# A hybrid RG-LRU and attention block: when the last two column tiles of x are read out, and where a weight's low part stands on VectorE

## The chip, the cores and the metric

The kernel runs on one core of a Trainium2 chip. The metric is the device time of one execution in microseconds (us). Engines are named as in the profile: PE is TensorE's matmuls and PEld its weight loads, DVE is VectorE, ACT is ScalarE, POOL is GpSimd, SP is SyncE, which here only issues DMAs. L503 is line 503 of the kernel.

## The reference, cut to what matters

One encoder layer over 512 positions of width 1024. The part around the change is the input projection, the four-tap depthwise convolution on its first 512 columns, and the two gates of the recurrence:

```python
h = rms_norm(x, attn_norm_g)
proj = h @ w_in
xr, gate, q, k, v = jnp.split(proj, [...], axis=-1)      # 512 columns each
y = b                                                     # centred depthwise convolution
for k in range(4):
    y = y + xp[:, k:k + S] * w[k]
# RG-LRU, forward and backward, each with its own gates; 8 blocks of 64 columns
r = sigmoid(einsum('bsnc,ncd->bsnd', xb, wa) + ba)
i = sigmoid(einsum('bsnc,ncd->bsnd', xb, wx) + bx)
a = exp(-8 * softplus(-lam) * r)
b_in = sqrt(1 - a * a) * (i * x)
# scan, gate with GeLU, dilated attention on q, k, v, two output projections,
# an MLP of width 4096 with squared ReLU, and a last RMSNorm
```

## The kernel before, in words

Every large matmul is made three times in a reduced-precision form of float32: each operand is split into a high part (`hi`) and a rest (`lo`), and `mm3` adds hi*hi, hi*lo and lo*hi (L333, L334, L335). Weights arrive by SP in chunks of 128x1024 (512 KB) into `wraw`, three buffers. `conv_hi(i)` makes chunk i's high part `whi`, on ACT (L277), or on DVE (L275) for chunks 7, 8 and 9. `conv_lo(i)` subtracts on DVE to make `wlo` (L285), which frees the `wraw` buffer, and asks SP for the next chunk (`emit_dma`, L241). Chunk 3 is the fourth column tile of x's weights, chunks 4 to 7 are V's, chunks 8 to 11 are the gate's.

Activations lie transposed: columns of the projection on the 128 partitions, the 512 positions along the free dimension. x's 512 columns are four tiles t = 0..3 (`pxr[t]`), each in a PSUM bank of its own. PSUM has eight banks; four are named `pj`, and `pxr[0..3]` take all four. The next users of these four are the four gate products `pg[0..3]` of a call of `lru_gates`, so a `pg` matmul has to wait until the `pxr` tile in its bank has been read out, and in the next call until ACT has read out the `pg` before it.

For each tile t the code has these steps:

- `conv_a(t)`: DVE reads `pxr[t]` out of PSUM and scales it into `xr` (L503), and ACT makes of it the convolution's first term `xc` (L505).
- `conv_b(t)`: three dependent DVE instructions add the other taps (L510, L511, L512), and SP copies the two halves of `xc` into each other's partitions (`xcs`, L522, two DMAs).
- `lru_gates(t)`: sixteen small matmuls (L531) from `xc` into four `pg` tiles, in the order 0, 2, 1, 3, and four sigmoids on ACT (L534) in the same order. The first sigmoid of the kernel has a load of ACT's function table ahead of it.

`xmm(ks)` issues the matmuls of x's fourth tile for the given parts k of the contraction. After them PE makes V in 32 steps n (three matmuls each; eight steps to a chunk, so step 8 is the first that uses chunk 5). `lru_gates(0..3)` stand behind steps 5, 8, 11 and 14; `conv_b(2)` behind step 2, `conv_b(3)` and `conv_lo(6)` behind step 6, `conv_hi(7)` and `conv_lo(7)` behind 7, `conv_hi(8)` and `conv_lo(8)` behind 12.

PE, ACT, DVE and POOL issue in the order in which the code is written. SP's order is laid out by the framework's planner. Each of them issues in order, so an instruction that waits holds up what stands behind it.

The lines that the change touches, as they are:

```python
xmm((0, 1))
rstd = row_tile(rcol, "et")
conv_a(0, pxr[0])
conv_a(1, pxr[1])
conv_hi(5)
cneg, chalf = next(spc)          # POOL: the last small constants
...                              # POOL: three DMA issues
xmm((2, 3, 4))
conv_b(0)
conv_lo(5)
conv_a(2, pxr[2])
xmm((5, 6))
conv_b(1)
conv_hi(6)
xmm((7,))
conv_a(3, pxr[3])
```

So DVE's order here is xr(0), xr(1), conv_b(0), wlo(5), xr(2), conv_b(1), xr(3), conv_b(2), conv_b(3), wlo(6), and ACT's is xc(0), xc(1), whi(5), xc(2), whi(6), xc(3), then the sigmoids.

Of the kernel before, what the change touches and what calls it, by code (L numbers as in the profile page):

```python
# [109 lines left out]
def hybrid_kernel(ctx: ExitStack, tc, xw, xn, w_in, w_v, w_out, w_up, w_dn, gates, vecs, rel, onehot, fg, out):  # L110
# [13 lines left out]
    def g_(name, dt=FT, shape=(P, S)):  # L124
        return work.tile(list(shape), dt, name=name, tag="g", bufs=NG)
# [4 lines left out]
    def ps_(name, tag):  # L130
        return psum.tile([P, S], FT, name=name, tag=tag, bufs={"pj": 4, "gs": 2, "et": 2}[tag])

    def f(t):
        return t.bitcast(FT)
# [5 lines left out]
    def vec(n, i):  # L140
        return vt[:, VEC[n] + i:VEC[n] + i + 1]
# [77 lines left out]
    def ublock(h, b, f):  # L219
        return w_up[h * HF + f + {"11": 0, "12": 1, "21": 2, "22": 3}[b]]  # L220
# [8 lines left out]
    def oblock(b, half=1):  # L229
        return w_out[int(half), int(b[1]) - 1, int(b[0]) - 1]  # L230

    def wblock(h, b, q):
        return w_dn[h, int(b[1]) - 1, (int(b[0]) - 1) * NQ + q]
# [3 lines left out]
    def emit_dma():  # L237
        if plain:
            i = plain.popleft()
            r = stream.tile([P, 1024], FT, name="wraw", tag="wraw", bufs=3)  # L240
            nc.sync.dma_start(r, source(chunks[i]))  # L241
            raws[i] = r
# [19 lines left out]
    def neg_next(i):  # L262
        conv_neg(i, stream.tile([P, 1024], FR, name="wlo", tag="wlo", bufs=4))

    def conv_hi(i):
        if i < len(chunks):
            i = swap.get(i, i)
            hi = stream.tile([P, 1024], FR, name="whi", tag="whi", bufs=4)
            if i + 1 == BY_DMA[2]:
                neg_next(i + 1)  # L270
            splits[i] = (hi,)
            if i in BY_DMA:
                splits[i] += (negs.pop(i),)
            if i in ON_DVE:
                nc.vector.tensor_copy(hi, raws[i])  # L275
            else:
                act(hi, raws[i], AF.Copy)  # L277

    def conv_lo(i):
        if i < len(chunks):  # L280
            i = swap.get(i, i)
            r = raws.pop(i)
            if i not in BY_DMA:
                lo = stream.tile([P, 1024], FR, name="wlo", tag="wlo", bufs=4)
                nc.vector.tensor_tensor(lo, r, f(splits[i][0]), op=OP.subtract)  # L285
                splits[i] += (lo,)
            c = chunks[i]
            if isinstance(c, tuple) and c[0] in ("o", "r"):
                if c[1][0] != "s":
                    emit_dma()  # L290
                elif c == ("r", "s2"):
                    nc.gpsimd.dma_start(r, oblock("21", 0), accum_op=OP.add)
                    raws[C_WO + RSEQ.index("s4")] = r
            elif isinstance(c, tuple) and len(c) == 4:
                h, kind, f0 = c[:3]
                if kind == "t1" and cq[h, f0, "t2"] not in raws:
                    nc.gpsimd.dma_start(r, ublock(h, "22", f0), accum_op=OP.add)
                    raws[cq[h, f0, "t2"]] = r
                elif kind == "22":
                    t = raws[cq[h, f0, "t3"]]  # L300
                    nc.vector.tensor_tensor(t, t, r, op=OP.add)
                elif kind in ("t2", "21"):
                    held[kind] = r
                    if len(held) == 2:
                        t = held.pop("t2")
                        nc.vector.tensor_tensor(t, t, held.pop("21"), op=OP.add)
                        raws[cq[h, f0, "t4"]] = t
                        emit_dma()
                if kind in ("11", "22"):
                    emit_dma()  # L310
            elif isinstance(c, tuple) and c[1][0] == "s":
                nxt = {"s1": ("s2", "22"), "s2": ("s4", "21")}.get(c[1])
                if nxt:
                    raws[cd_[c[0]] + {"s2": 2 * NQ + 2 * c[2], "s4": 6 * NQ + c[2]}[nxt[0]]] = r
                    if (c[0], c[1]) != (1, "s2"):
                        nc.gpsimd.dma_start(r, wblock(c[0], nxt[1], c[2]), accum_op=OP.add)
            else:
                emit_dma()
# [13 lines left out]
    def mm3(o, a, b, first, last, on=False):  # L332
        nc.tensor.matmul(o, lhsT=a[0], rhs=b[0], start=bool(first), stop=False, skip_group_check=on)  # L333
        nc.tensor.matmul(o, lhsT=a[0], rhs=b[1], start=False, stop=False, skip_group_check=on)  # L334
        nc.tensor.matmul(o, lhsT=a[1], rhs=b[0], start=False, stop=bool(last), skip_group_check=on)  # L335
# [66 lines left out]
    def hk(k):  # L402
        return (h_hi[:, k, :], h_lo[:, k, :])

    def wk(c, k):
        if c < 3:
            return tuple(t[:, c * P:(c + 1) * P] for t in w3[k])
        hi, lo = splits[c]
        return (hi[:, k * P:(k + 1) * P], lo[:, k * P:(k + 1) * P])
# [31 lines left out]
    pxr = {t: ps_("pxr", "pj") for t in range(3)}  # L441
# [59 lines left out]
    def conv_a(t, pp):  # L501
        xr = g_("xr")
        nc.vector.tensor_tensor(xr, pp, rstd, op=OP.mult)  # L503
        c = g_("xc")
        act(c, xr, AF.Identity, scale=vec("w2", t), bias=vec("cb", t))  # L505
        xrt[t], xc[t] = xr, c

    def conv_b(t):
        xr, c = xrt.pop(t), xc[t]
        stt(c[:, 2:], xr[:, :S - 2], vec("w0", t), c[:, 2:], op0=OP.mult, op1=OP.add)  # L510
        stt(c[:, 1:], xr[:, :S - 1], vec("w1", t), c[:, 1:], op0=OP.mult, op1=OP.add)  # L511
        stt(c[:, :S - 1], xr[:, 1:], vec("w3", t), c[:, :S - 1], op0=OP.mult, op1=OP.add)  # L512
        xcs[t] = swapped("xcs", c)
# [5 lines left out]
    def swapped(name, t):  # L519
        o = g_(name)  # L520
        for b in range(2):
            nc.sync.dma_start(o[halves[1 - b]], t[halves[b]])  # L522
        return o
# [134 lines left out]
    def xmm(ks):  # L658
        for k in ks:
            mm3(pxr[3], wk(3, k), hk(k), k == 0, k == KD - 1)  # L660
# [4 lines left out]
    rstd = row_tile(rcol, "et")  # L665
    conv_a(0, pxr[0])
    conv_a(1, pxr[1])
    conv_hi(5)
    cneg, chalf = next(spc)
    nc.gpsimd.dma_start(relt, rel)  # L670
# [1 line left out]
        nc.gpsimd.dma_start(oht[i], onehot[:, BCOL[i]])  # L672
    xmm((2, 3, 4))
    conv_b(0)
    conv_lo(5)
    conv_a(2, pxr[2])
    xmm((5, 6))
    conv_b(1)
    conv_hi(6)
    xmm((7,))  # L680
    conv_a(3, pxr[3])


    scans = deque()
# [1177 lines left out]
```

## Time and profile before

| what | value |
|---|---|
| median of 3 runs | 528.62 us (528.49 to 528.72) |
| profiled execution | 528.4 us, its span 526.6 us |
| granted TensorE clock, mean | 0.997 |
| busy: PE, PEld, DVE, ACT, POOL | 519.5, 446.8, 431.0, 361.1, 67.5 us |
| V's first step on PE | starts at 28.57 us of the span |
| the four groups of gate matmuls | start at 32.74, 37.11, 41.67 and 45.82 us |

The span is the time from the first instruction to the last; the 1.8 us around it are not in the trace. Matmuls overlap: a matmul row lasts some 0.39 us, but the next one starts 0.23 us later. Where PE is followed closely, the distance between starts counts and not the duration. DVE and ACT rows overlap a little in the same way, by up to 0.1 us.

### The profile page before, as it was taken

To read this page: it belongs to the slowest core of one execution; us is meant where nothing else is said; L and a number is where in the kernel's file an instruction comes from. 1 tells how busy PE (TensorE), PEld (TensorE's weight loads), DVE (VectorE), ACT (ScalarE), POOL (GpSimd) and SP (SyncE) were. 2 spreads that over 40 slices of the span, in tenths; PEclk is the share of its full clock that TensorE was granted. 3 is DMA by queue.
4 is the path that set the end of the run, shared out by engine and by line. 5 is a ranking of instruction groups with operands and counts; after the bars stand their busy time and mean duration, and the time that the engine had idled before them with its cause. 6 is when DMAs were issued, how large, how long until landed. Compare 5 with 4: busy or idle time off the path is not lost.

```text
span 526.6 us, 9183 instructions
## 1 busy us (share of the span) xinstructions
PE 519.5 (99%) x3495; PEld 446.8 (85%) x3495; DVE 431.0 (82%) x710; ACT 361.1 (69%) x570; POOL 67.5 (13%) x96
## 2 busy tenths in 40 slices
PE   9999999999999999999999999999999999999995
PEld 7866888787877888899999888888999999888884
DVE  5799589778789898898779987889756977987885
ACT  7577967777878958585577755566477677656654
POOL 1631000001002121001300132001101300213000
PEclk9999999999999999999999999999999999999998
DMA  8888155585478999948494999976978496899604
GB/s 308 285 210 221 41 158 160 172 153 180 91 241 178 315 223 256 356 153 200 118 225 137 241 265 273 281 300 160 288 232 201 115 228 202 219 276 250 149 1 159
DMA packets 35739, 108.29 MB, mean 206 GB/s; under 512 B 4109, under 2 KB 7082, under 8 KB 35696
## 3 DMA queue, kind: packets, MB, share of 16 engines
q1 hardware_dynamic: 26000, 74.67, 41.1%
q0 software_dynamic: 8784, 31.76, 32.5%
q10 hardware_dynamic: 912, 1.28, 1.3%
q8 instruction: 27, 0.44, 0.4%
q14 instruction: 16, 0.13, 0.1%
HBM read 98.24 MB, written 4.21 MB: 195 GB/s over the span
## 4 chain that ended last, share of the span: by engine, by line
PE 98%; DMA 1%; DVE 0%; ACT 0%; issue 0%; ACTq 0%
PE pu L335 10%; PE pu L334 10%; PE pu L333 10%; PE pd L334 10%; PE pd L333 10%; PE pd L335 10%; PE pqk L333 3%; PE pqk L335 3%; PE pqk L334 3%; PE pt L853 2%; PE pav L940 2%; PE pxr L446 2%; PE pv L333 2%; PE pg L531 2%; PE pn L799 1%; PE pv L335 1%
## 5 line engine op out<-in xcount | busy, mean ns | idle before, releaser
L285 DVE TENSOR_TENSOR wlo<-wraw,whi 128x1024 fp32r<-128x1024 f32 x72 | 87.8, 1220 | 24.7 <-ACT whi L277 24.5
L277 ACT ACTIVATE whi<-wraw 128x1024 fp32r<-128x1024 f32 x69 | 72.9, 1058 | 36.1 <-PE pd L335 21.6
L334 PE MATMUL pd<-wlo,ah 128*128 128x512 f32 (+1 forms) x195 | 75.2, 386 | 0.0
L333 PE MATMUL pd<-whi,ah 128*128 128x512 f32 (+1 forms) x195 | 75.2, 386 | 0.0
L335 PE MATMUL pd<-whi,al 128*128 128x512 f32 (+1 forms) x195 | 75.2, 386 | 0.0
L277 ACT ACTIVATE whi<-tw 128x1024 fp32r<-128x1024 f32 x40 | 42.3, 1059 | 37.7 <-DMA tw<-in_w_up_dram 10.7
L285 DVE TENSOR_TENSOR wlo<-tw,whi 128x1024 fp32r<-128x1024 f32 x40 | 48.9, 1222 | 18.6 <-ACT whi L277 18.6
L334 PE MATMUL pu<-hl,whi 128*128 128x256 f32 x224 | 63.4, 283 | 0.0
L335 PE MATMUL pu<-hh,wlo 128*128 128x256 f32 x224 | 63.4, 283 | 0.0
L333 PE MATMUL pu<-hh,whi 128*128 128x256 f32 x224 | 63.4, 283 | 0.0
L333 PE MATMUL pu<-h2h,whi 128*128 128x256 f32 (+1 forms) x200 | 60.1, 300 | 0.0
L335 PE MATMUL pu<-h2h,wlo 128*128 128x256 f32 (+1 forms) x200 | 60.0, 300 | 0.0
L334 PE MATMUL pu<-h2l,whi 128*128 128x256 f32 (+1 forms) x200 | 60.0, 300 | 0.0
L333 PEld LDWEIGHTS pu<-hh,whi 128*128 128x128 f32 x224 | 43.0, 192 | 0.0
L334 PEld LDWEIGHTS pu<-hl,whi 128*128 128x128 f32 x224 | 43.0, 192 | 0.0
L335 PEld LDWEIGHTS pu<-hh,wlo 128*128 128x128 f32 x224 | 43.0, 192 | 0.0
L333 PEld LDWEIGHTS pd<-whi,ah 128*128 128x128 f32 x195 | 36.6, 188 | 7.4
L335 PEld LDWEIGHTS pd<-whi,al 128*128 128x128 f32 x195 | 36.6, 188 | 7.3
L334 PEld LDWEIGHTS pd<-wlo,ah 128*128 128x128 f32 x195 | 36.6, 188 | 7.3
L277 ACT ACTIVATE whi<-ts 128x1024 fp32r<-128x1024 f32 x24 | 25.5, 1061 | 22.6 <-PE pd L335 19.5
L334 PEld LDWEIGHTS pu<-h2l,whi 128*128 128x128 f32 x200 | 38.3, 191 | 1.3
L333 PEld LDWEIGHTS pu<-h2h,whi 128*128 128x128 f32 x200 | 38.3, 191 | 1.3
(296 smaller groups left out, 1223.8 us busy)
## 6 DMA issues: line engine op xcount, KB each, us to landing
wraw<-in_w_up_dram SPq DMA_DIRECT2D x25, 512.0 KB
ts<-in_w_dn_dram POOLq DMA_DIRECT2D x24, 512.0 KB, 10.6
wraw<-in_w_dn_dram SPq DMA_DIRECT2D x24, 512.0 KB
tw<-in_w_up_dram SPq DMA_DIRECT2D x15, 512.0 KB
tw<-in_w_up_dram POOLq DMA_DIRECT2D x15, 512.0 KB, 7.4
wraw<-in_w_in_dram SPq DMA_DIRECT2D x13, 512.0 KB
ts<-in_w_dn_dram SPq DMA_DIRECT2D x8, 512.0 KB
tw<-in_w_dn_dram SPq DMA_DIRECT2D x8, 512.0 KB
```

The source lines that it names most:

```text
L277: act(hi, raws[i], AF.Copy)
L285: nc.vector.tensor_tensor(lo, r, f(splits[i][0]), op=OP.subtract)
L333: nc.tensor.matmul(o, lhsT=a[0], rhs=b[0], start=bool(first), stop=False, skip_group_check=on)
L334: nc.tensor.matmul(o, lhsT=a[0], rhs=b[1], start=False, stop=False, skip_group_check=on)
L335: nc.tensor.matmul(o, lhsT=a[1], rhs=b[0], start=False, stop=bool(last), skip_group_check=on)
L446: nc.tensor.matmul(pxr[t], lhsT=wk(t, k)[a], rhs=hk(k)[b], start=k == 0 and i == 0, stop=False)
L531: nc.tensor.matmul(pg[2 * d + j][halves[b ^ d]], lhsT=gwr[t][halves[b], c], rhs=xc[t][halves[b]], start=True, stop=True)
L799: nc.tensor.matmul(pnear[p][e][r, o:o + k1 - k0], lhsT=q, rhs=raw[p, 1][halves[e], k0:k1], start=u == u0, stop=True, skip_group_check=True)
L853: nc.tensor.transpose(pt[:, i * P:(i + 1) * P], en[h][u][:, c * P:(c + 1) * P], ident)
L940: nc.tensor.matmul(o(half[e]), lhsT=v[:, h * DH:(h + 1) * DH], rhs=c(et[h, x]), start=first, stop=last, skip_group_check=True)
```

## The change

`conv_a(2)` moves ahead of `conv_hi(5)`, next to `conv_a(0)` and `conv_a(1)`. The matmuls of x's fourth tile keep their order; `conv_a(3)` moves ahead of `conv_b(1)` and ahead of `conv_hi(6)`. `conv_lo(5)` moves behind `conv_b(1)`. No instruction is added or removed.

```diff
     conv_a(0, pxr[0])
     conv_a(1, pxr[1])
+    conv_a(2, pxr[2])
     conv_hi(5)
     cneg, chalf = next(spc)
     nc.gpsimd.dma_start(relt, rel)
...
     xmm((2, 3, 4))
     conv_b(0)
+    xmm((5, 6, 7))
+    conv_a(3, pxr[3])
+    conv_b(1)
     conv_lo(5)
-    conv_a(2, pxr[2])
-    xmm((5, 6))
-    conv_b(1)
     conv_hi(6)
-    xmm((7,))
-    conv_a(3, pxr[3])
```

DVE's order becomes xr(0), xr(1), xr(2), conv_b(0), xr(3), conv_b(1), wlo(5), conv_b(2), conv_b(3), wlo(6). ACT's becomes xc(0), xc(1), xc(2), whi(5), xc(3), whi(6), then the sigmoids.

## The prediction, made before the result was known

> **What bounds the kernel now.** I read the page's head, its busy times and its chain first.
>
> ```profile
> span 526.6 us, 9183 instructions
> ...
> PE 519.5 (99%) x3495; PEld 446.8 (85%) x3495; DVE 431.0 (82%) x710; ACT 361.1 (69%) x570; POOL 67.5 (13%) x96
> ...
> PE 98%; DMA 1%; DVE 0%; ACT 0%; issue 0%; ACTq 0%
> ```
>
> The chain that ended last is 98% PE. The change removes no instruction, so it can only shorten stretches in which PE waits. I looked for such stretches in PE's timeline from the fourth x tile to the last group of gate matmuls (columns: start, duration, both in us).
>
> ```profile
> 28.34 0.39 PE L335 MATMUL pxr<-h_hi,wlo 128*128 128x512 f32 x1
> ...
> 32.74 2.14 PE L531 MATMUL pg<-xc,gwr 64*64 64x512 f32 x16
> 34.81 0.50 PE L333 MATMUL pv<-whi,h_hi 128*128 128x512 f32 x1
> ...
> 36.55 0.40 PE L334 MATMUL pv<-wlo,h_hi 128*128 128x512 f32 x1
> ...
> 37.11 2.35 PE L531 MATMUL pg<-xc,gwr 64*64 64x512 f32 x16
> 39.39 0.50 PE L333 MATMUL pv<-whi,h_hi 128*128 128x512 f32 x1
> ...
> 41.67 1.95 PE L531 MATMUL pg<-xc,gwr 64*64 64x512 f32 x16
> 43.55 0.50 PE L333 MATMUL pv<-whi,h_hi 128*128 128x512 f32 x1
> ...
> 45.82 1.95 PE L531 MATMUL pg<-xc,gwr 64*64 64x512 f32 x16
> 47.70 0.50 PE L333 MATMUL pv<-whi,h_hi 128*128 128x512 f32 x1
> ```
>
> The same sixteen matmuls stand here four times. From the group's start to the next V matmul it is 2.07, 2.28, 1.88 and 1.88 us. The last two agree, so 1.88 is the undisturbed price; tile 0's group loses 0.19 and tile 1's 0.40 us, 0.59 together. The weight loads' waits and timeline name who holds tile 1's group (in brackets: idle time before the row, and what ended it).
>
> ```profile
> PEld pg L531 <- ACT ga L534: 0.6, 2, 0.4
> ...
> 38.38 0.19 PEld L531 LDWEIGHTS pg<-xc,gwr 64*64 64x64 f32 x4 [0.23 <-ACT ga L534]
> ```
>
> The 0.6 is idle time of the weight loads, part of which they have in an undisturbed group too; the starts above give the loss to PE. Next, DVE and ACT in that stretch.
>
> ```profile
> 25.29 1.29 DVE L503 TENSOR_TENSOR xr<-pxr,rrow 128x512 f32<-128x512 f32 x2 [2.62 <-ACT rrow L432]
> 26.86 0.75 DVE L510 SCALAR_TENSOR_TENSOR xc<-xr,vt,xc 128x510 f32<-128x510 f32 x1 [0.29 <-ACT xc L505]
> ...
> 28.43 0.75 DVE L512 SCALAR_TENSOR_TENSOR xc<-xr,vt,xc 128x511 f32<-128x511 f32 x1
> 29.10 1.22 DVE L285 TENSOR_TENSOR wlo<-wraw,whi 128x1024 fp32r<-128x1024 f32 x1
> 30.24 0.69 DVE L503 TENSOR_TENSOR xr<-pxr,rrow 128x512 f32<-128x512 f32 x1
> 30.84 0.74 DVE L510 SCALAR_TENSOR_TENSOR xc<-xr,vt,xc 128x510 f32<-128x510 f32 x1
> ...
> 33.07 0.68 DVE L503 TENSOR_TENSOR xr<-pxr,rrow 128x512 f32<-128x512 f32 x1
> ...
> 38.14 1.22 DVE L285 TENSOR_TENSOR wlo<-wraw,whi 128x1024 fp32r<-128x1024 f32 x1
> ```
>
> ```profile
> 26.01 1.52 ACT L505 ACTIVATE xc<-xr,vt 128x512 f32<-128x512 f32 x2 [0.76 <-DVE xr L503]
> 27.44 1.04 ACT L277 ACTIVATE whi<-wraw 128x1024 fp32r<-128x1024 f32 x1
> ...
> 33.79 0.81 ACT L505 ACTIVATE xc<-xr,vt 128x512 f32<-128x512 f32 x1 [1.07 <-DVE xr L503]
> 34.62 1.28 ACT L534 ACT_TABLE_LOAD   x1
> 35.91 4.80 ACT L534 ACTIVATE ga<-pg,vt 128x512 f32<-128x512 f32 x8
> 42.85 2.42 ACT L534 ACTIVATE ga<-pg,vt 128x512 f32<-128x512 f32 x4 [2.14 <-PE pg L531]
> ```
>
> Both losses come from one row, the xr at 33.07. It reads the fourth x tile out and ends at 33.75. Tile 0's group started at 32.74 and in half of its time reaches the bank that this row frees: that is the 0.19. Behind it stand, one after the other on ACT, xc(3) at 33.79, the table load at 34.62 and the sigmoids at 35.91. Four sigmoids last 2.42 us (row 42.85), so tile 0's last `pg` bank comes free at 35.91 + 2.42 = 38.33, and tile 1's group, begun at 37.11, waits for it until 38.38: that is the 0.40.
>
> **The change part by part.** *DVE.* Distances between starts, from the rows: an xr 0.60 (30.24 to 30.84), a conv_b 2.24 (26.86 to 29.10, three instructions), a wlo 1.14 (29.10 to 30.24). The new order from 25.29: three xr to 27.09. By then xc(0) is there: its wait ended at 26.86, and the 0.29 of that wait is filled by xr(2). conv_b(0) to 29.33. xr(3) from 29.33: PE's last matmul for it starts at 28.34 and ends at 28.73, so it waits for nothing and ends at 29.33 + 0.68 = 30.01 instead of 33.75. conv_b(1) from 29.93 to 32.17. wlo(5) from 32.17 to 32.17 + 1.22 = 33.39 instead of 30.32; DVE goes on at 33.31. conv_b(2) and conv_b(3), 4.48 together, to 37.79, where wlo(6) starts, 0.35 earlier than 38.14.
>
> *ACT.* An xc takes 0.72 between starts ((27.44 - 26.01) / 2), a whi 1.04, an end-to-start step 0.02 to 0.04. xc(2) from 27.44 (its xr ends at 25.29 + 1.20 + 0.69 = 27.18), whi(5) from 28.16 to 29.20, three us before wlo(5) reads it. xc(3) at 30.05, whi(6) at 30.77 to 31.81, the table load at 31.83 to 33.11. The first sigmoid then waits for PE: it starts 1.18 after its group in the undisturbed case (41.67 to 42.85), so at 33.92, and the fourth ends at 33.92 + 2.42 = 36.34.
>
> *PE.* Tile 0's group starts at 32.74 as before; its four banks are free from 30.01 on and xc(0) since about 29.4, so it takes 1.88 and V goes on at 34.62. Tile 1's group starts 0.19 earlier, at 36.92. The banks are free from 36.34, xc(1) has been complete since 32.3, so it takes 1.88 too. Gain 0.19 + 0.40 = 0.59 us. The term is bounded by zero (both stalls stay) and 0.59 (PE has nothing else to lose in these groups); I take the upper end, since the nearest check, 36.34 against 36.92, leaves 0.58 us, and the last bank is needed later still.
>
> *What the moved steps hold up.* wlo(5), 3.07 us later, is first used by V's step 8: the row 36.55 above, 36.36 after the gain. Ready at 33.39, it leaves 2.97 us. It costs nothing as long as that cover stands. Its `wraw` buffer and the load that follows come later too. SP's timeline:
>
> ```profile
> 30.58 0.53 SPq L241 DMA_DIRECT2D wraw<-in_w_in_dram  x1
> ...
> 33.18 6.21 SPq L522 DMA_DIRECT2D xcs<-xc  x6
> ```
>
> The slowest kind of 512 KB load in the page's DMA issues (last column: median us from issue to landing), and DVE's timeline around the cast that reads the chunk:
>
> ```profile
> tw<-in_w_dn_dram POOLq DMA_DIRECT2D x8, 512.0 KB, 12.0
> ```
>
> ```profile
> 43.55 0.69 DVE L275 CAST whi<-wraw 128x1024 fp32r<-128x1024 f32 x1
> ...
> 58.30 0.69 DVE L565 SCALAR_TENSOR_TENSOR ga<-la,ga 128x512 f32<-128x512 f32 x1 [6.13 <-ACT ga L554]
> ```
>
> On SP the load (the gate's first chunk) now stands behind tile 1's two xcs copies and behind wlo(5): about 33.45 instead of 30.58. The cast that reads it comes at 43.20 (43.55 less 0.35), 9.75 us after the issue. The trace has no landing time for SP's loads. The kind shown takes 12.0 us (POOL's, which add into memory that holds data already); by that, DVE would wait 2.25 us and still have the 6.13 us of idle time ahead of the row 58.30. So zero at both ends. The xcs copies of tiles 2 and 3 queue behind this load instead of ahead of it in part; they are read by DVE after 45 us, and the same 6.13 us cover them. POOL's three issues and PE's matmuls keep their order.
>
> *Sum.* 528.4 - 0.59 = 527.8 for an execution like the profiled one. The median of the runs is 0.22 above that execution, so 528.62 - 0.59 = 528.03 against the median. This is 0.11% less; this kernel's runs spread by 0.23, and about 0.2% (1.06 us) is what I call distinguishable, so I forecast no change in that sense, with a small true gain.
>
> *A rule against the change.* POOL issues DMAs at the place where DVE now does its moved work (its timeline):
>
> ```profile
> 27.77 0.84 POOL L670 DMA_DIRECT2D relt<-in_rel_dram  x1
> ...
> 29.73 1.00 POOL L1062 DMA_DIRECT2D tw<-in_w_out_dram  x1
> ```
>
> From the first to the end of the last it is 27.77 to 30.73, 2.96 us. The tap at 28.43 lies beside them and took 0.75; the one at 30.84, with POOL just done, took 0.74. So I charge nothing. The Trainium skill, "SBUF — State Buffer", section "Who interferes with whom", says that a DVE instruction with two SBUF inputs shares a read port with GpSimd under an exclusive lock, so that one blocks the other fully. In the strictest form of that, all 2.96 us would be lost to DVE, wlo(5) would be ready at 36.35, and V's step 8 at 36.36 would just not wait: the sum would stay 528.03 with nothing to spare. The durations just shown do not agree with such a block.
>
> **The rivals.** *Given back later.* PE comes 0.59 earlier to work that is paced by loads, and waits there. Views of the groups and of the weight loads' waits over the whole span:
>
> ```profile
> L277 ACT ACTIVATE whi<-tw 128x1024 fp32r<-128x1024 f32 x40 | 42.3, 1059 | 37.7 <-DMA tw<-in_w_up_dram 10.7
> ```
>
> ```profile
> PEld pav L940 <- ACT e L841: 0.7, 2, 0.4
> ...
> PEld pt L853 <- ACT whi L277: 0.3, 1, 0.3
> ...
> PEld pn L799 <- DVE e L823: 0.2, 1, 0.2
> ```
>
> For it: ACT does wait 10.7 us for loads in the MLP. Against it: PE's weight loads have one single wait after these groups that names a converted weight, 0.3 us long; later loads are asked for by DVE's conv_lo, so they come earlier along with it. Time: 528.6.
>
> *More than the sum.* After the gate groups eight kinds of released wait are left (first and last above), 3.0 us together. If the shift brought half of them into cover, 1.5 us more: 526.5. For it nothing but that they exist; against it, all eight wait for DVE or ACT work that is itself triggered by PE and moves along.
>
> *Slower: wlo(5) comes late.* Place: V's step 8 on PE. It decides from 2.97 us of extra delay in DVE's row of seven instructions and the wlo, and then costs one to one. To be slower than before it needs 3.56, by over 0.2% 4.62 us: 529.7 at that point. For it: the wlo's end moves by 3.07 us, and DVE has no idle time in that row to catch up in. Against it: the eight instructions are known to the hundredth, and PE's order of work ahead of xr(3) does not change.
>
> **How the numbers follow.** The forecast gets 0.68, given back 0.17, more than the sum 0.09, slower 0.06. Predicted time 528.0. Of the forecast I leave 0.02 beyond 0.2% faster, for waits that close by chance: faster 0.11, same 0.66 + 0.17 = 0.83, slower 0.06. The range reaches from 527.5, the forecast less half a us for such waits, to 528.8, given back plus the runs' spread; it holds the forecast and the first rival, 0.85 less their tails.
>
> **What would show it.** Right: both first gate groups at 1.88 us from start to next V matmul; the fourth xr near 29.3 and the table load near 31.8; no wait of PE at step 8; the fourth gate group's start 0.59 earlier (45.23 instead of 45.82), and that shift kept to the end. Wrong: a wait of the gate matmuls for xc or ACT, a PE wait ahead of V's `wlo` matmul, a DVE wait ahead of the cast near 43.2 that outlasts 6 us, or a shift that is there at 60 us and gone at 500.

## The result and the profile after

| kernel | median us | runs |
|---|---|---|
| before | 528.47 (527.97 to 528.88) | 22 |
| changed | 527.75 (527.26 to 528.24) | 22 |

The ratio is 0.9984, 95% interval 0.9978 to 0.999. A second comparison, on the chip of the first four experiments, gave 527.73 (11 runs) against 528.36 (33 runs), ratio 0.9991, interval 0.9983 to 1.0, which just reaches no change. So the change saves 0.6 to 0.7 us, 0.12% to 0.14% by the medians. The page's head of the changed kernel's profile:

```profile
span 526.0 us, 9184 instructions
...
PE 518.8 (99%) x3495; PEld 446.1 (85%) x3495; DVE 431.2 (82%) x710; ACT 361.6 (69%) x570; POOL 67.4 (13%) x96
```

The span is 0.6 us shorter, PE's busy time 0.7 us, with the same number of PE instructions. PE's timeline around the first two groups of gate matmuls (start, duration, in us):

```profile
32.84 1.95 PE L531 MATMUL pg<-xc,gwr 64*64 64x512 f32 x16
34.72 0.50 PE L333 MATMUL pv<-whi,h_hi 128*128 128x512 f32 x1
...
36.44 0.39 PE L334 MATMUL pv<-wlo,h_hi 128*128 128x512 f32 x1
...
36.98 1.95 PE L531 MATMUL pg<-xc,gwr 64*64 64x512 f32 x16
38.86 0.50 PE L333 MATMUL pv<-whi,h_hi 128*128 128x512 f32 x1
```

From start to the next V matmul both groups take 1.88 us, where they took 2.07 and 2.28. The weight loads' waits for all four groups name no ACT any more:

```profile
PEld pg L531 <- issue: 3.6, 12, 0.4
```

These twelve idle pieces, three to a group, belong to the undisturbed group. DVE and ACT in the same stretch:

```profile
25.39 1.89 DVE L503 TENSOR_TENSOR xr<-pxr,rrow 128x512 f32<-128x512 f32 x3 [2.61 <-ACT rrow L432]
27.19 0.74 DVE L510 SCALAR_TENSOR_TENSOR xc<-xr,vt,xc 128x510 f32<-128x510 f32 x1
27.97 0.75 DVE L511 SCALAR_TENSOR_TENSOR xc<-xr,vt,xc 128x511 f32<-128x511 f32 x1
28.76 0.75 DVE L512 SCALAR_TENSOR_TENSOR xc<-xr,vt,xc 128x511 f32<-128x511 f32 x1
29.43 0.68 DVE L503 TENSOR_TENSOR xr<-pxr,rrow 128x512 f32<-128x512 f32 x1
...
32.26 1.22 DVE L285 TENSOR_TENSOR wlo<-wraw,whi 128x1024 fp32r<-128x1024 f32 x1
...
37.85 1.22 DVE L285 TENSOR_TENSOR wlo<-wraw,whi 128x1024 fp32r<-128x1024 f32 x1
```

```profile
26.12 2.23 ACT L505 ACTIVATE xc<-xr,vt 128x512 f32<-128x512 f32 x3 [0.76 <-DVE xr L503]
28.25 1.05 ACT L277 ACTIVATE whi<-wraw 128x1024 fp32r<-128x1024 f32 x1
30.14 0.82 ACT L505 ACTIVATE xc<-xr,vt 128x512 f32<-128x512 f32 x1 [0.85 <-DVE xr L503]
30.87 1.04 ACT L277 ACTIVATE whi<-wraw 128x1024 fp32r<-128x1024 f32 x1
31.93 1.28 ACT L534 ACT_TABLE_LOAD   x1
33.97 2.42 ACT L534 ACTIVATE ga<-pg,vt 128x512 f32<-128x512 f32 x4 [0.75 <-PE pg L531]
```

In the last row's brackets, ACT now waits 0.75 us for PE, where before PE waited for ACT.

### The profile page after: what moved, and what is told of

Same layout as the page of the kernel before. It is cut to its first block, busy times and chain, and to the rows that moved or that the text cites. A ratio compares the mean times of both kernels' runs of the same rounds, so it can differ in the third digit from the quotient of the medians.

```text
span 526.0 us, 9184 instructions
## 1 busy us (share of the span) xinstructions
PE 518.8 (99%) x3495; PEld 446.1 (85%) x3495; DVE 431.2 (82%) x710; ACT 361.6 (69%) x570; POOL 67.4 (13%) x96
## 4 chain that ended last, share of the span: by engine, by line
PE 97%; DMA 1%; DVE 0%; ACT 0%; SPq 0%; issue 0%; ACTq 0%
PE pu L333 10%; PE pu L335 10%; PE pu L334 10%; PE pd L335 10%; PE pd L333 10%; PE pd L334 10%; PE pqk L333 3%; PE pqk L335 3%; PE pqk L334 3%; PE pt L852 2%; PE pav L939 2%; PE pv L333 2%; PE pg L531 1%; PE pn L798 1%; PE pv L334 1%; PE pv L335 1%
## 5 line engine op out<-in xcount | busy, mean ns | idle before, releaser
L335 PEld LDWEIGHTS pu<-h2h,wlo 128*128 128x128 f32 x200 | 38.3, 191 | 1.3
```

## The experiments

The theory: the 0.59 us are two separate stalls of PE behind one late instruction, the read-out of x's fourth tile. 0.19 us hang on its PSUM bank, 0.40 us on ACT, which loads the sigmoids' table only behind that tile's first term. The rivals: that the place of the weight rest matters, that there is only one stall, and that the gain is taken back later.

In the text below, a group's time is the distance from its first matmul to the next V matmul, and a shift is the difference in start of the same matmul between a kernel's profile and that of before.

### The changed kernel again

> The changed kernel itself, beside the three edits that follow. By the theory (the fourth x tile's read-out decides, 0.19 us through its PSUM bank and 0.40 us through ACT's sigmoids) 0.6 us below the kernel before. If the further 0.13 us by which the two medians of the result differ are real, 0.7 us.

> A third profile of the changed kernel: both gate groups at 1.88 us again; the shift against before at V's first step may be anywhere within half a us, as in the profiles so far, and the shift from there to the end is 0.6 us again unless a wait near 420 us comes up here too.

Measured: 527.73 against 528.36 us, 0.63 below; the third profile's one run took 527.55, beside one run of before at 527.82. Both groups took 1.88 us each time. In the three profiles of the changed kernel, PE's shift from the start of the first group to 519 us went from +0.10 to -0.58, from -0.28 to -0.93 and from -0.20 to -0.85: 0.65 to 0.68 us, and from 48 us on it moved by no more than 0.02. The groups make 0.59 of it. The V matmuls between the groups also ran a little shorter: from the V matmul behind one group to the next group it is 2.26 us twice (34.72 to 36.98, and 38.86 to 41.12), where the rows of before have 2.30 and 2.28. That is 0.06 more.

### The fourth tile alone

```diff
     conv_b(0)
     conv_lo(5)
     conv_a(2, pxr[2])
-    xmm((5, 6))
+    xmm((5, 6, 7))
+    conv_a(3, pxr[3])
     conv_b(1)
     conv_hi(6)
-    xmm((7,))
-    conv_a(3, pxr[3])
```

> Only the fourth tile's read-out moves ahead of the second convolution; the second weight rest of V and the third tile stay where they were before. Theory: xr(3) starts at 30.8, the table load at 33.5, the fourth sigmoid ends at 37.2, its bank is needed at about 37.8; both gate groups take 1.88 us, the whole 0.59 us below before, equal to the changed kernel. Rival (the weight rest has to leave the convolutions' way): ACT stays late, the second gate group still waits, 0.2 us below before.

Measured: 527.78 against 528.36 us, ratio 0.9992 (0.9983 to 1.0001), 0.05 from the changed kernel's median. PE and ACT:

```profile
32.65 1.95 PE L531 MATMUL pg<-xc,gwr 64*64 64x512 f32 x16
34.53 0.50 PE L333 MATMUL pv<-whi,h_hi 128*128 128x512 f32 x1
...
36.79 1.95 PE L531 MATMUL pg<-xc,gwr 64*64 64x512 f32 x16
38.67 0.50 PE L333 MATMUL pv<-whi,h_hi 128*128 128x512 f32 x1
```

```profile
33.36 1.28 ACT L534 ACT_TABLE_LOAD   x1
34.65 2.42 ACT L534 ACTIVATE ga<-pg,vt 128x512 f32<-128x512 f32 x4
```

Both groups take 1.88 us, although the sigmoids end at 37.07, 0.28 after the second group has begun: the last bank is needed later than the first. So this one move carries the whole gain, and the moves of the third tile and of the weight rest add nothing that can be measured. In this profile the weight loads' waits in the gate groups still name ACT's `xc` (0.4 us) and DVE's `xc` (0.3 us), with no loss to PE: the distance between starts tells of a loss, and a name alone does not.

In this profile 0.56 us were lost again near 420 us, in the MLP:

```profile
PEld pu L335 <- DVE wlo L285: 0.5, 1, 0.5
```

> A second profile of the kernel in which only the fourth tile's read-out moves. In the first profile its PE shift against before was 0.75 us up to 400 us of the span and 0.22 behind a wait for a weight rest near 420 us. If that wait belongs to the kernel, it is there again; if it belongs to one execution (the medians of this edit and of the full change differ by 0.05 us), it is gone and the shift behind the gate groups is kept to the end.

The second profile (one run, 527.71 us, beside one of before at 527.82) has no such wait: its shift is -0.70 at 48 us and at 519 us. So it comes in single executions of this kernel, and no other profile here has it; the rival "given back later" was seen as an event and not as a steady part of the change. The traces show where the rest's lateness came from: in the first profile ACT's conversion of a chunk that it waits for from DMA starts at 403.40, in the second at 401.22, and DVE's rest that PE waited for starts 2.18 us later too, at 419.61 against 417.43. What made that load late was not tried.

### The weight rest alone

```diff
     conv_b(0)
-    conv_lo(5)
     conv_a(2, pxr[2])
     xmm((5, 6))
     conv_b(1)
+    conv_lo(5)
     conv_hi(6)
     xmm((7,))
     conv_a(3, pxr[3])
```

> Only the weight rest moves behind the second convolution; both read-outs stay behind it. Theory: xr(3) starts at 33.07 as before, so the gate groups take 2.07 and 2.28 us again, 0.0 us against before. Rival (the rest's place matters): first group at 1.88, 0.2 us or more below before.

Measured: 528.36 against 528.36 us, ratio 0.9999 (0.9991 to 1.0008). DVE and PE:

```profile
31.59 1.22 DVE L285 TENSOR_TENSOR wlo<-wraw,whi 128x1024 fp32r<-128x1024 f32 x1
32.73 0.68 DVE L503 TENSOR_TENSOR xr<-pxr,rrow 128x512 f32<-128x512 f32 x1
```

```profile
32.38 2.17 PE L531 MATMUL pg<-xc,gwr 64*64 64x512 f32 x16
34.47 0.50 PE L333 MATMUL pv<-whi,h_hi 128*128 128x512 f32 x1
...
36.74 2.38 PE L531 MATMUL pg<-xc,gwr 64*64 64x512 f32 x16
39.06 0.50 PE L333 MATMUL pv<-whi,h_hi 128*128 128x512 f32 x1
```

The read-out still stands behind everything else and starts 0.35 after the first group; the groups take 2.09 and 2.32 us. Exchanging two pieces of work ahead of the late instruction does not make it earlier.

### One stall or two

Here DVE's read-out stays late, and only ACT's first term of the fourth tile moves behind the first tile's sigmoids.

```diff
     xmm((7,))
-    conv_a(3, pxr[3])
+    conv_a3_dve()                 # xr(3) alone
...
         if n in GATES:
             lru_gates(GATES[n])
+            if n == 5:
+                conv_a3_act()     # xc(3)
```

> The kernel before, with only ACT's first term of the fourth tile moved behind the first tile's sigmoids; DVE's read-out stays late. Theory: two separate stalls. The first group keeps its 2.07 us (bank), the sigmoids start at 34.1 and the second group takes 1.88: 0.40 us below before. Rival (one stall, both by the late read-out): 2.07 and 2.28, 0.0 us.

Measured: 528.12 against 528.36 us, ratio 0.9993 (0.9985 to 1.0002). The times alone don't separate this from no change, nor quite the fourth tile alone; the profiles do:

```profile
32.50 2.15 PE L539 MATMUL pg<-xc,gwr 64*64 64x512 f32 x16
34.58 0.50 PE L333 MATMUL pv<-whi,h_hi 128*128 128x512 f32 x1
...
36.85 1.95 PE L539 MATMUL pg<-xc,gwr 64*64 64x512 f32 x16
38.73 0.50 PE L333 MATMUL pv<-whi,h_hi 128*128 128x512 f32 x1
```

The first group keeps its stall (2.08 us), the second has lost its own (1.88 us). The shift goes from -0.24 at the first group to -0.68 at 519 us, 0.44 of gain. So there are two stalls, and the second hangs on ACT's order and not on the bank that the read-out frees. No wait in the profile of before names the read-out as what holds the first group. That it does so rests on the runs: the first stall stays where the read-out stays late (here and with the weight rest alone), and is gone where the read-out is early.

### How late ACT may be

The changed kernel with four, then six copies of 128x512 on ACT ahead of the table load:

```diff
     conv_hi(6)
+    pad = g_("pad")
+    for _ in range(4):            # 6 in the second kernel
+        act(pad, f(h_hi)[:, 0, :], AF.Copy)
```

> The changed kernel with four more copies on ACT (128x512, some 0.52 us each, 2.1 together) ahead of the table load. Theory: the sigmoids start at 35.3 instead of 33.97, the fourth ends at 37.7, its bank is needed 0.9 us into the second group, at 37.9: no stall, as the changed kernel, 0.6 us below before. Rival (PE needs all four banks when its group starts, at 36.98): a stall of 0.7 us, 0.1 us above before.

> The same with six copies, 3.1 us. Theory: the sigmoids start at 36.3, the fourth ends at 38.7 against 37.9 needed: the second group loses 0.9 us, 0.3 us above before. Rival (all four banks at the start): 1.8 us, 1.2 us above before. Rival (ACT does not matter once the read-out is early): 0.6 us below before.

Measured: 528.09 against 528.42 us with four (ratio 0.9993, 0.9984 to 1.0003) and 529.63 with six (1.0022, 1.0013 to 1.0032). ACT and PE, first with four copies, then with six:

```profile
31.61 2.61 ACT L683 ACTIVATE pad<-h_hi 128x512 f32<-128x512 f32 x4
...
35.53 4.79 ACT L534 ACTIVATE ga<-pg,vt 128x512 f32<-128x512 f32 x8
```

```profile
36.78 2.31 PE L531 MATMUL pg<-xc,gwr 64*64 64x512 f32 x16
39.02 0.50 PE L333 MATMUL pv<-whi,h_hi 128*128 128x512 f32 x1
```

```profile
32.29 3.93 ACT L683 ACTIVATE pad<-h_hi 128x512 f32<-128x512 f32 x6
...
37.54 4.74 ACT L534 ACTIVATE ga<-pg,vt 128x512 f32<-128x512 f32 x8
```

```profile
33.32 1.95 PE L531 MATMUL pg<-xc,gwr 64*64 64x512 f32 x16
...
38.28 2.81 PE L531 MATMUL pg<-xc,gwr 64*64 64x512 f32 x16 [0.75 <-ACT ga L534]
41.02 0.50 PE L333 MATMUL pv<-whi,h_hi 128*128 128x512 f32 x1
```

Both expectations missed: with four copies no stall was expected and there is one, and with six it is larger. A copy took 0.65 us (2.61 / 4) and not 0.52. With that the theory holds. With four copies the fourth sigmoid ends at 35.53 + 2.42 = 37.95 and the second group loses 2.24 - 1.88 = 0.36, so the last bank was wanted at 37.59, 0.81 us into the group. With six it ends at 39.96; the group, which without a wait begins 4.14 us behind the first (32.84 to 36.98 in the changed kernel), would begin at 37.46 and want the bank at 38.27: a loss of 1.69. Measured, 41.02 - 33.32 = 7.70 against 6.02 (32.84 to 38.86): 1.68. Up to that point ACT's lateness is free, past it one microsecond costs one.

The two stalls of before give the same point, from rows that the prediction shows: 33.75 - 0.19 - 32.74 = 0.82 for the first group's bank, and 38.33 - 0.40 - 37.11 = 0.82 for the second's. So it could be read off before any run.

The median with six copies, 1.21 us above before, is what the rival (all four banks at the group's start) had forecast, but with copies that were put too short. With 0.65 us each, that rival asks for losses of 37.95 - 36.78 = 1.17 and 39.96 - 37.46 = 2.50, where 0.36 and 1.68 were measured, and with six copies the group starts at 38.28, ahead of the fourth sigmoid's end. That rival does not hold, and neither does the one by which ACT no longer matters (0.6 us below before).

### The weight rest too late

The changed kernel with the rest moved on behind the fourth convolution:

```diff
     conv_b(1)
-    conv_lo(5)
     conv_hi(6)
...
             conv_b(3)
+            conv_lo(5)
             conv_lo(6)
```

> The changed kernel with the weight rest of V's second chunk moved on behind the fourth convolution. Theory: the rest is ready at 37.95, V's step 8 wants it at 36.44; PE waits 1.55 us, nothing gives it back: 0.95 us above before. Rival (PE's loss is taken up by later waits): less than 0.5 us above before.

Measured: 529.42 against 528.42 us, ratio 1.0017 (1.0008 to 1.0027). DVE and PE:

```profile
36.14 2.35 DVE L285 TENSOR_TENSOR wlo<-wraw,whi 128x1024 fp32r<-128x1024 f32 x2
```

```profile
35.63 0.39 PE L333 MATMUL pv<-whi,h_hi 128*128 128x512 f32 x1
37.41 0.50 PE L334 MATMUL pv<-wlo,h_hi 128*128 128x512 f32 x1 [1.40 <-DVE wlo L285]
```

The first of the two rests ends at 36.14 + 1.22 = 37.36 and PE goes on at 37.41. The distance of the two matmuls is 1.78 instead of 0.23, a loss of 1.55, as expected, and the shift of +0.59 at 48 us is there at 519 us. So the slower rival has the place and the price that the prediction gave it; the change itself just stays away from its point.

## Why the prediction was right

- *The sum.* 0.59 was forecast; the groups gave exactly that, and the stretch 0.65 to 0.68. The 0.06 in the V matmuls between the groups was not in the sum, and why they are shorter was not tried. The median came out at 527.75 instead of 528.03; 0.15 of the 0.28 is that the kernel before, with 22 runs, stands at 528.47 and not at 528.62. The spread of 0.23 that the range was built on came from three runs; 22 runs of the same kernel spread by 0.91.
- *DVE's and ACT's steps.* This execution was 0.10 us late ahead of the change. Less that, xr(3) starts at 29.33 as forecast, the weight rest ends at 33.38 (forecast 33.39), the table load starts at 31.83 (31.83), the sigmoids start at 33.87 (33.92). Distances between starts, and not durations, made these agree: with the durations the four xr rows alone would put the weight rest 4 x 0.09 = 0.36 us too late.
- *The margin for the second group.* I took the start of the group as the time when ACT must be done, and noted that the last bank is needed later. The copies showed how much: 0.81 us.
- *The weight rest's cover.* Forecast 2.97 us, in the profile 36.44 - 33.48 = 2.96.
- *SP.* The one step that failed: the gate's first load was to be issued at about 33.45 and was issued at 34.19, because the four xcs issues ahead of it kept SP until 34.09. The last pair of them began at 32.40 and took 1.69 us, where the same pair took 1.11 in the profile of before; why was not tried.

```profile
29.57 4.52 SPq L522 DMA_DIRECT2D xcs<-xc  x4
34.19 0.54 SPq L241 DMA_DIRECT2D wraw<-in_w_in_dram  x1
```

```profile
43.18 0.69 DVE L275 CAST whi<-wraw 128x1024 fp32r<-128x1024 f32 x1
```

  The cast that reads it ran at 43.18, with no wait shown ahead of it, so this cost nothing.
- *The rule on GpSimd and DVE.* The tap at 27.97 and the one behind it, beside POOL's DMA issues, took 0.75 us each, like the row 28.43 of before: DVE did not pay, as the sum assumed. POOL did, in the changed kernel's timeline:

```profile
26.98 0.23 POOL L182 TENSOR_SCALAR cneg<-sp 128x8 f32<-128x8 f32 x1
27.30 0.73 POOL L183 TENSOR_SCALAR chalf<-sp 128x8 f32<-128x8 f32 x1
```

  The second of these two like instructions runs beside the tap at 27.19 and takes 0.73 instead of 0.23 us. That much agrees with the Trainium skill, "SBUF — State Buffer", "Who interferes with whom", that the two share a port; nothing waited for it here. It is not shown that the port is the cause: in the profile of before both instructions start beside the tap at 26.86, and the first still took 0.23 us, the second 0.52.
- *What was not needed.* I costed the three moves as one. The fourth tile's read-out alone brings the gain; the rest is neutral, as far as these runs can tell.

## What to carry to other kernels

Before you move work off a busy engine, look for the instruction that frees a PSUM bank for the next product, and for the first instruction behind which a table load stands: here one 0.68 us read-out held up PE twice, through two different engines. A moved weight conversion is free exactly until the matmul that reads it, and then costs one to one; both points can be read from the trace of before by adding up distances between starts. When a gain is a tenth of a per cent, follow the shift of the same matmul through two profiles; by the medians alone, 22 runs of each kernel separated it here, and 11 against 33 did not quite.

## What was not expected of the hardware

The spread of whole runs, about 1 us (527.26 to 528.24), has the size of a spread that arises ahead of the change. PE's work ahead of its first gate group is the same in all these kernels, yet that group began anywhere between these two rows (the kernel with the late rest, and the one with six copies):

```profile
32.26 1.95 PE L531 MATMUL pg<-xc,gwr 64*64 64x512 f32 x16
```

```profile
33.32 1.95 PE L531 MATMUL pg<-xc,gwr 64*64 64x512 f32 x16
```

That is 1.06 us over the eleven profiles, and whatever the group started with was kept to the end within 0.03 us, apart from what the edits themselves add and the one wait near 420 us. The traces show where most of it arises: of the 1.06 us between these two profiles, 0.73 are there by 10 us of the span. Up to there PE's weight loads wait for ACT's conversions of x's first weights (`w3h`, L367 and L374) 0.7 us in the one and 1.4 us in the other, and ACT in turn waits for loads from `in_xw_dram`, 0.3 and 1.7 us. What makes these loads vary was not tried.
